# A hybrid decoder layer on one core: the order of the instructions is set by another machine model

## The chip, the core and the metric

The kernel runs on one core of a Trainium2 chip. The metric is the device time of one execution in microseconds (us); the time before is the median of three runs. A core has a matrix engine (TensorE, PE in the profile; its weight loads are shown apart as PEld), VectorE (DVE), ScalarE (ACT), GpSimd (POOL) and SyncE (SP). Each engine takes its instructions strictly in the order in which they stand in its queue and waits at each for the semaphores it needs. Transfers between the chip's memory and the core's on-chip memory are issued from the queues of SP, ACT and POOL.

## The reference

One layer for two groups of tokens at once: a prompt of 512 tokens, and a sample group of 8 sequences with 4 new tokens each, 544 tokens in all, 1024 channels, everything in float32.

```
z = rms_norm(x) @ w_in                                  # 1024 x 3080
za, zb, zc = split(z)
ya = rwkv7(za)            # a recurrence over the tokens, 4 heads of 64
yb = fox(zb)              # attention with forget gates, 8 heads of 64; the prompt over itself,
                          # the sample over 2048 old keys and values in pages of 128 (page_table)
yc = conv_module(zc)      # gated causal convolution of width 31
x += concat(ya, yb, yc) @ w_out
mk, mv = memory(mem_prompt @ w_xk, mem_prompt @ w_xv)   # 256 memory tokens
x += cross_attention(rms_norm(x) @ w_xq, mk, mv) @ w_xo # 4 heads of 256
x += (silu(conv(gate)) * conv(val)) @ w_down            # gate, val = rms_norm(x) @ w_up, 2816 wide
```

The keys, values, gates, states and convolution tails are outputs too.

## The kernel before

The weight products keep the tokens on the free axis: 128 output channels by 272 (or 512) tokens accumulate in one PSUM bank over eight blocks of 128 input channels. Each float32 factor is split into a high and a low part (`split`, L244), and three matmuls make one product of them, high by high, high by low and low by high. `weights` (L267) loads blocks of columns of a weight, ScalarE makes the high part (`w_hi`), VectorE the low (`w_lo`, L247). All matmuls go through `mm` (L185, recorded as L186), transpositions on TensorE through `tr` (L214, L216).

The stages, by the names that the profile and the order show:

- The first product, `bank_g<-act_h` and `act_l` (z = x @ w_in), with three streams beside it: the recurrence's chunks (`rwkv_recurrence`, L896; small matmuls of 64x64 into `bank_r`, on `zbuf`, `RA`, `TR`, `WU`, `G`), the convolution's taps, and the normalisation of keys and queries.
- The prompt's attention, four pairs of heads (`attend`, L1305): scores into `bank_r`, their exponentials in `S0` and `S1`, the transposed weights `PT`, the values.
- The sample's attention over the old keys, one sequence after the other (`sample_past`, L1703). An indirect transfer fetches four pages of keys into `w_raw` (1 MB, two buffers; `four_pages`, L1387, recorded as L1389), VectorE transposes it in blocks of 32 into `KT` (L1404), and 16 matmuls of 128x32 tiles give scores in `bank_s` (`past_scores`, L1394). The values come as `page` (three buffers), and 4 matmuls per page add to `bank_v` (`past_values`, L1448). There are 32 transfers of keys and 32 of values.
- The memory's keys and values, `bank_g<-xT` (`memory`, L1526; the memory's operand lies where the residual `xT` is later), then the output projection of the mixer, `bank_g<-four` with w_out (`out_prompt`, L1629).
- Cross attention: from the first `bank_d` (the query product with w_xq) on. Then the feed-forward, again in `bank_g`.

The program is recorded as several generators side by side. `weave` (L346) takes the next step of the one that is least far along; L1241 weaves the first product, recurrence and convolution, L1726 the sample's attention with everything else up to the output projection (`rest`, L1576). That recording is only a proposal. A scheduler in the library goes through the recorded instructions, and at each step takes, of those that are ready by its own model of the machine, the one of the highest priority, which is the recording position minus what `tc.high_priority(n)` adds. So `urgent` (L350) sets its steps before `n` instructions of the others:

```
def urgent(steps, ahead):
    while True:
        with tc.high_priority(ahead):
            step = next(steps, None)
```

The recurrence is recorded with `ahead` 800 (L1240), the sample's attention with 0 (L1726). `pinned` (L181) can keep instructions in recorded order. Which engine does a copy recorded as `nc.any.tensor_copy` (`anycp`: L1330, L1439, L1524, L1640 and others) is the scheduler's choice as well, and so are the buffer numbers and the semaphore waits that follow from the order.

Of the kernel before, what the change touches and what calls it, by code (L numbers as in the profile page):

```python
# [8 lines left out]
F32 = mybir.dt.float32  # L9
# [34 lines left out]
def _consts():  # L44
    """What depends on shapes alone: identities, masks, selections."""
# [46 lines left out]
    # rows (head, page of four, query) against pages, queries and columns of the like  # L92
# [18 lines left out]
def _past_consts():  # L111
    """of rows (head, page of four, query): causal mask, selections of pages, queries and columns"""
# [14 lines left out]
def _cross_consts():  # L127
    """of rows (head of two, 64 of the keys, token) those of a head and the 64; then selections of 32 rows, four times over"""
    p, m = np.arange(128)[:, None], np.arange(8)[None, :]
    own = [(m // 4 == h) & (m % 4 == p // 32) for h in range(2)]  # L130
    four = [p == 32 * x + np.arange(128)[None, :] % 32 for x in range(4)]
    return np.concatenate(own + four, 1).astype(np.float32)
# [5 lines left out]
def _pack_vectors(x):  # L138
    """Per-channel vectors side by side, a column for each 128 channels."""
# [15 lines left out]
def hybrid_step(tc, A):  # L155
# [62 lines left out]
    def rsqrt_from(out, in_, scale, eps):  # L218
        """out = (in * scale + eps) ** -0.5 by the logarithm and the exponential"""
        act(out=out, in_=in_, func=AF.Ln, scale=scale, bias=eps)  # L220
        act(out=out, in_=out, func=AF.Exp, scale=-0.5)

    def half_xyy(t, y, x, scale, eps):
        """t = (x * scale + eps) / 2 * y ** 2 for y, about the inverse root: (1.5 - t) * y is that root to the last bits"""
# [3 lines left out]
    def rsqrt_rows(out, x, n, scale, eps, eps_ap, work):  # L228
        """out = (x * scale + eps) ** -0.5 for n numbers to a partition"""
# [6 lines left out]
    def neg_sigmoid(t, e):  # L236
        """-1 / (1 + exp(-t)) in place, for t >= -40; by a Newton step"""
# [6 lines left out]
    def split(h, l, src, tt=vtt):  # L244
        """src = h + l exactly, both float32r"""
        acopy(h, src)
        tt(out=l, in0=src, in1=h.bitcast(F32), op=SUB)  # L247

# [18 lines left out]
    def weights(src, kb, cols, width=128, raws=None):  # L267
        """loads blocks of columns, two at most, and returns how to split each"""
# [37 lines left out]
    def gemm_steps(src, cols, xh, xl, evac, bank, spans=EVEN, kb=8, ahead=0, raws=None, first=None):  # L306
        """evac(ps, i, a) for span a of the i-th block of 128 columns; yields what each step costs TensorE"""
# [22 lines left out]
    def woven(*streams, first=False):  # L330
        """several streams side by side, each (its steps, their cost in all, where it sets in), in proportion; to the end of
        all or of the first"""
# [17 lines left out]
    def urgent(steps, ahead):  # L350
        """the steps, each before that many instructions of the others"""
# [27 lines left out]
    # what outlives the phases  # L379
# [16 lines left out]
    def four_blocks(n, dtype=F32R):  # L396
        """the places of four blocks of an operand, high or low"""
        return (yfp, yrp, xkp, xvp)[n].tile([128, 4, NT], dtype, name="four")

    yF = four_blocks(0, F32)  # first holds FoX's queries  # L400
# [5 lines left out]
    cum = cpl.tile([128, SEQ], F32R, name="cum")  # high parts from 0 and 64, low ones from 32 and 96  # L406
# [10 lines left out]
    # ================= inputs, first norm =================  # L417
# [20 lines left out]
    def norm_tok(xt, n, gain, ss, h, l, lo, work, bank, junk):  # L438
        """rows of xt, normed, transposed and split into columns lo.. of h and l"""
# [11 lines left out]
    # the operand is not yet divided by its root mean square: that follows after the products  # L451
# [4 lines left out]
    def roots(lo, n):  # L456
        """1 / root mean square of tokens lo .. lo + n, on all partitions"""
# [43 lines left out]
    # ================= gates of the cached keys =================  # L501
    # one row for each (batch, page), then (batch, head) by key, cumulated from the end
# [28 lines left out]
    # ================= RWKV columns, shifted by a token as they come =================  # L531
# [48 lines left out]
    # ================= RWKV: gates, keys, as their columns come =================  # L580
# [4 lines left out]
    def rmm(lhsT, rhs, evac):  # L585
        """float32 product with all 544 tokens of rhs, by halves"""
# [17 lines left out]
    def gates():  # L604
        """yields how many blocks of columns the next step needs"""
        yield 2
        # tanh(t) = 2 / (1 + exp(-2 t)) - 1
# [6 lines left out]
        # t1: minus the sigmoid of w, t4: that of a  # L614
# [6 lines left out]
        # decays: cumulated in each chunk, centred on half of the chunk's total  # L621
# [7 lines left out]
        # the step to the next chunk's centre, where that chunk's state will lie: [other half, block, head]  # L629
# [11 lines left out]
        # unit keys  # L641
# [40 lines left out]
    # where the cached keys and values lie: of four pages each, partition (page, k) takes rows 4 k .. 4 k + 3  # L682
# [13 lines left out]
    # ================= FoX and conv columns =================  # L696
# [9 lines left out]
    def finish(n=1):  # L706
        """what was put off until n more evacuations"""
# [5 lines left out]
    def evac_fl(ps, i, a):  # L713
        """forget gate: log_sigmoid(y) = -(max(-y, 0) + ln(1 + exp(-|y|)))"""
# [35 lines left out]
    def tok_major(dst, dst_s, src, src_s):  # L750
        """[128 channels, tokens] -> the prompt's token rows and the sample's"""
# [88 lines left out]
    def conv_taps():  # L840
        """the prompt's convolution: some taps on VectorE, the others by ScalarE and GpSimd"""
# [18 lines left out]
    def conv_ahead():  # L860
# [22 lines left out]
        for m in range(2):  # L883
            # the sample's windows, all taps at once: [batch * token, tap], by half the batches
# [11 lines left out]
    def rwkv_recurrence():  # L896
        def group_norm(y, n, heads, ps, work):
            """ps [n, heads, 64] -> y, each row of 64 centred and scaled"""
# [17 lines left out]
        # ================= RWKV: inverses of the blocks of 16 on the diagonals =================  # L916
        # N of (head, block of 128 tokens) as [chunk of two, block of 16, row] by column; with DVE's transposes by blocks
        # of 32 each of the 128 triangles comes to a partition (chunk, half, block of two, head and block of tokens)
# [48 lines left out]
        # ================= RWKV: sample, rows (head, batch, token) =================  # L967
        def sample_steps(rk, rk2):
# [43 lines left out]
            # -alpha S0 and rho S0, each row with its own batch  # L1012
# [37 lines left out]
            # the state after the four tokens  # L1050
# [18 lines left out]
        # ================= RWKV: chunks of 64, two to a block of 128 tokens =================  # L1069
# [4 lines left out]
        def chain(i, j, out):  # L1074
            """what a block and two heads need that no state enters, step by step"""
# [23 lines left out]
            # inverse of I - N by doubling blocks, from those of 16  # L1099
# [43 lines left out]
        def four(t, i):  # L1143
            """a block's columns as [head of two, its block, 64]"""
            return t[:, :, i * 128: (i + 1) * 128].rearrange("p j (r t) -> p j r t", r=2)

        def stateless(i):
            """of a block, in the places of what entered: AT (beta), RP (kap), the outputs (ynT) and the state (values) but for
            what the state before adds"""
# [36 lines left out]
        def stateful(i):  # L1186
            """the state, chunk after chunk: that of chunk ch lies in half ch % 2"""
# [51 lines left out]
    # what of the recurrence is left then runs beside the sample's attention  # L1239
# [38 lines left out]
    def recurrence_end():  # L1278
        """RWKV's group: ((norm * g + b) + bonus) * gate"""
# [9 lines left out]
        # where the residual will lie, the memory's operand  # L1289
# [3 lines left out]
        # causal mask, after nothing for the keys before  # L1293
# [7 lines left out]
    # ================= FoX: the prompt's attention, two heads at a time =================  # L1301
# [895 lines left out]
```

## Time and profile before

| what | value |
|---|---|
| time, median of 3 runs | 1304.64 us (1300.55 to 1308.29) |
| span of the profiled execution, which is its own time from first to last instruction | 1301.6 us |
| TensorE busy; weight loads busy | 1234.1 us; 1011.6 us |
| VectorE, ScalarE, GpSimd busy | 809.1, 501.2, 290.6 us |
| matmul records | 10410 |
| moved by DMA | 173.83 MB, 134 GB/s in the mean |

The span lies 3.0 us under the median. Busy shares are means over stages of different kinds: the first product (to about 320 us), attention of prompt and sample (about 320 to 460), memory and output projection with the rest of the sample's attention (about 460 to 698), cross attention (698 to about 890), feed-forward (to the end). A matmul of float32 data can leave two records in the trace, so the records (10410) are more than the program's matmuls (8376).

### The profile page before, as it was taken

The numbers are of one execution on the slowest core, as the hardware profiler recorded it, in microseconds if no ns is written. First come the engines' busy times: TensorE is split into PE (matmuls) and PEld (weight loads), VectorE is DVE, ScalarE is ACT, GpSimd is POOL, SyncE is SP. The second block draws the span as 40 slices with busy tenths as digits, with TensorE's granted clock in tenths as the row PEclk, the third lists the DMA queues.
The fourth block names the chain that finished last, engine by engine and source line by source line (L and its number), as shares of the span: only waits on it lengthen the run. The fifth ranks groups of instructions, "written<-read, shape, count | busy, mean of one in ns | idle before, by whom it ended". The sixth has DMA issues, their size and how long they took to land.

```text
span 1301.6 us, 24852 instructions
## 1 busy us (share of the span) xinstructions
PE 1234.1 (95%) x10410; PEld 1011.6 (78%) x10410; DVE 809.1 (62%) x1514; ACT 501.2 (39%) x996; POOL 290.6 (22%) x322
## 2 busy tenths in 40 slices
PE   7899899999899999999998988999999999999997
PEld 6788788875555467654447875799999999999996
DVE  4699998765777377453234677557767424777631
ACT  5454543341456435221242422335444323444321
POOL 1262430033342131112223242012111100111120
PEclk9999999997699999999998998999999999999999
DMA  7221220221788497576663465033322323222231
GB/s 227 59 65 51 50 75 19 67 87 44 268 304 304 155 306 244 198 231 226 218 215 118 151 232 174 23 103 98 98 93 60 93 73 127 68 96 88 76 111 48
DMA packets 129649, 173.83 MB, mean 134 GB/s; under 512 B 7029, under 2 KB 110981, under 8 KB 121336
## 3 DMA queue, kind: packets, MB, share of 16 engines
q0 software_dynamic: 15216, 84.80, 18.1%
q1 hardware_dynamic: 88160, 70.76, 17.9%
q10 hardware_dynamic: 26160, 16.66, 4.4%
q8 instruction: 82, 1.34, 0.4%
q14 instruction: 31, 0.25, 0.1%
HBM read 164.54 MB, written 7.88 MB: 132 GB/s over the span
## 4 chain that ended last, share of the span: by engine, by line
PE 77%; DVE 9%; issue 5%; ACT 4%; DMA 3%; POOL 2%; SPq 0%; POOLq 0%; ACTq 0%; DVEq 0%
PE bank_g L186 42%; PE bank_r L186 10%; PE bank_d L186 6%; PE bank_s L186 6%; PE bank_v L186 4%; PE bank_a L186 2%; PE bank_r L216 2%; DVE w_lo L247 1%; PE bank_t L216 1%; PE bank_x L216 1%; DMA w_raw<-in_w_in_dram 1%; DMA w_raw<-in_w_out_dram 1%; DVE four L855 1%; DVE KT L1404 1%; ACT w_hi L177 1%
## 5 line engine op out<-in xcount | busy, mean ns | idle before, releaser
L186 PE MATMUL bank_g<-four,w_hi 128*128 128x272 f32 (+1 forms) x1536 | 284.7, 301 | 2.7 <-ACT w_hi L177 2.0
L177 ACT CAST w_hi<-w_raw 128x1024 fp32r<-128x1024 f32 (+3 forms) x149 | 140.6, 946 | 269.8 <-PE bank_g L186 206.1
L186 PEld LDWEIGHTS bank_g<-four,w_hi 128*128 128x128 f32 x1536 | 222.1, 189 | 26.4 <-issue 19.9
L247 DVE TENSOR_TENSOR w_lo<-w_raw,w_hi 128x1024 fp32r<-128x1024 f32 (+3 forms) x149 | 164.0, 1103 | 87.2 <-ACT w_hi L177 78.2
L186 PE MATMUL bank_g<-four,w_lo 128*128 128x272 f32 (+1 forms) x768 | 173.4, 301 | 0.5 <-DVE w_lo L247 0.5
L186 PEld LDWEIGHTS bank_g<-four,w_lo 128*128 128x128 f32 x768 | 122.1, 189 | 11.3 <-issue 8.6
L186 PE MATMUL bank_g<-act_h,w_hi 128*128 128x272 f32 (+2 forms) x400 | 124.6, 312 | 6.2 <-ACT w_hi L177 2.8
L186 PE MATMUL bank_g<-act_h,w_lo 128*128 128x272 f32 (+2 forms) x400 | 122.9, 308 | 0.0
L186 PE MATMUL bank_g<-act_l,w_hi 128*128 128x272 f32 (+2 forms) x400 | 122.0, 305 | 0.0
L2108 POOL TENSOR_SCALAR ysm<-HS,vec 128x32 f32<-128x32 f32 x44 | 42.0, 954 | 255.1 <-ACT HS L177 255.1
L1404 DVE STREAM_TRANSPOSE KT<-w_raw 128x2048 f32<-128x2048 f32 x32 | 73.5, 2302 | 23.9 <-PE bank_s L186 22.8
L186 PEld LDWEIGHTS bank_g<-act_h,w_hi 128*128 128x128 f32 x400 | 79.5, 199 | 10.5 <-ACT w_hi L177 3.2
L186 PEld LDWEIGHTS bank_g<-act_h,w_lo 128*128 128x128 f32 x400 | 79.1, 198 | 2.8 <-issue 1.2
L186 PEld LDWEIGHTS bank_g<-act_l,w_hi 128*128 128x128 f32 x400 | 79.4, 198 | 2.3 <-issue 1.1
L186 PE MATMUL bank_s<-KT,w_hi 128*32 128x128 f32 x1024 | 76.6, 292 | 3.4 <-DVE rsq L226 1.7
L186 PE MATMUL bank_d<-four,w_hi 128*128 128x272 f32 x384 | 78.1, 299 | 0.0
L186 PE MATMUL bank_g<-in_h,w_hi 128*128 128x272 f32 x352 | 73.6, 290 | 0.0
L186 PE MATMUL bank_g<-in_l,w_hi 128*128 128x272 f32 x352 | 73.5, 290 | 0.0
L186 PE MATMUL bank_g<-in_h,w_lo 128*128 128x272 f32 x352 | 73.2, 289 | 0.0
L186 PE MATMUL bank_v<-page,w_lo 128*32 128x512 f32 x256 | 67.8, 603 | 1.8 <-DMA page<-in_cache_fox_v_dram,kidx 1.8
L186 PEld LDWEIGHTS bank_s<-KT,w_hi 128*32 128x32 f32 x1024 | 39.2, 115 | 32.5 <-issue 19.8
L186 PEld LDWEIGHTS bank_d<-four,w_hi 128*128 128x128 f32 x384 | 61.9, 193 | 1.0
(631 smaller groups left out, 2458.6 us busy)
## 6 DMA issues: line engine op xcount, KB each, us to landing
w_raw<-in_w_up_dram SPq DMA_DIRECT2D x20, 1024.0 KB, 5.1
w_raw<-in_w_down_dram SPq DMA_DIRECT2D x16, 704.0 KB, 4.7
w_raw<-in_w_in_dram SPq DMA_DIRECT2D x17, 512.0 KB, 4.2
w_raw<-in_cache_mem_k_dram SPq DMA_DIRECT2D x16, 512.0 KB, 5.0
sV<-in_cache_mem_v_dram POOLq DMA_DIRECT2D x12, 512.0 KB, 6.4
w_raw<-in_w_in_dram SPq DMA_DIRECT2D x4, 1024.0 KB, 6.6
w_raw<-in_w_xk_dram ACTq DMA_DIRECT2D x8, 512.0 KB, 10.6
w_raw<-in_w_xv_dram ACTq DMA_DIRECT2D x8, 512.0 KB, 10.7
```

Of the source, the lines that this page charges most:

```text
L177: nc.scalar.copy(out, in_)
L186: pinned(nc.tensor.matmul(out, lhsT, rhs, start=start, stop=stop, skip_group_check=True))
L216: pinned(nc.tensor.transpose(out=out, in_=in_, identity=ident[p0:p0 + k, p0:p0 + k]))
L247: tt(out=l, in0=src, in1=h.bitcast(F32), op=SUB)
L855: vstt(out=yp, in0=U[:, m, w: w + SEQ], scalar=w_tap, in1=yp, op0=MUL, op1=ADD)
L1404: nc.vector.transpose(out=KT, in_=K)
L2108: nc.gpsimd.tensor_scalar(out=ysm, in0=H[:, 2:6, 1:], scalar1=w[2], scalar2=b, op0=MUL, op1=ADD)
```

## The change

One argument is added where the kernel's context is made; the scheduler then orders the same recorded instructions against a model that follows the queues and the transfers in time. The diff also takes out the docstrings and comments, with the line numbers kept; two of those places stand for all.

```diff
     def urgent(steps, ahead):
-        """the steps, each before that many instructions of the others"""
+
...
-    with tile.TileContext(nc) as tc:
+    with tile.TileContext(nc, schedule_with_timeline_sim=True) as tc:
         hybrid_step(tc, A)
```

The set of instructions stays: 8376 matmuls, 64 indirect transfers, and so on. 37 of the copies that any engine may do go from VectorE to ScalarE (net; 25 of them at L1439). What changes is the order on each engine and the waits. Counted over the orders: changes of tile shape between neighbouring matmuls fall from 700 to 397, those between 128x32 and 128x128 tiles from 403 to 153; runs of a single key matmul (`bank_s<-KT`) from 98 to 2, of a single value matmul (`bank_v<-page`) from 40 to 4. Of the key matmuls, 224 stood after the memory's first matmul and none do now; of the value matmuls 91, and none now. Of the recurrence's 540 matmuls of 64x64, all stood ahead of the last matmul of the first product and 84 do now.

TensorE's queue in the output projection before; `bank_g` is the projection, `KT` old keys, `page` old values (the last number is a run of equal rows):

```order
L186 MATMUL bank_s_6317<-KT_6324,w_hi_6318 32x128
L186 MATMUL bank_g_6448<-four_5944,w_hi_6449 128x512
L186 MATMUL bank_s_6317<-KT_6324,w_hi_6318 32x128
L186 MATMUL bank_g_6448<-four_5933,w_lo_6450 128x512
L186 MATMUL bank_s_6317<-KT_6324,w_hi_6318 32x128 x3
L186 MATMUL bank_g_6579<-four_5933,w_hi_6580 128x512
L186 MATMUL bank_s_6317<-KT_6324,w_hi_6318 32x128
L186 MATMUL bank_v_6342<-page_6503,w_lo_5995 32x512
```

And where the same keys, `KT_6324`, stand now, between transpositions (`ident`) of the prompt's attention weights `S0` and `S1`:

```order
L216 MATMUL bank_r1_4115<-ident_59,page_4095 128x128 x4
L216 MATMUL bank_r2_4147<-ident_59,S0_4007 128x128 x4
L186 MATMUL bank_s_6317<-KT_6324,w_hi_6318 32x128 x16
L186 MATMUL bank_s_6317<-KT_6390,w_hi_6318 32x128 x14
L216 MATMUL bank_r0_4153<-ident_59,S1_4008 128x128 x4
L186 MATMUL bank_s_6317<-KT_6390,w_hi_6318 32x128 x2
L186 MATMUL bank_v_6055<-page_6056,w_lo_5456 32x512 x4
L216 MATMUL bank_r2_4230<-ident_59,S1_4008 128x128 x3
L186 MATMUL bank_s_6317<-KT_6420,w_hi_6318 32x128 x14
```

The single key matmuls have become runs of 14 and 16, and they no longer stand among the projection's.

TensorE's queue at the first key tiles now, inside the recurrence (`zbuf`, `G`, `TR`, `RA`, `beta`):

```order
L186 MATMUL bank_r1_1816<-beta_389,RA_388 64x64 x2
L186 MATMUL bank_r0_1829<-zbuf0_1305,G0_1751 64x64 x2
L186 MATMUL bank_r0_1829<-zbuf0_1305,G1_1808 64x64 x2
L186 MATMUL bank_r1_1837<-zbuf1_1308,G2_1760 64x64 x2
L186 MATMUL bank_r1_1837<-zbuf1_1308,G3_1817 64x64 x2
L186 MATMUL bank_s_3676<-KT_3727,w_hi_3677 32x128 x15
L186 MATMUL bank_r0_1829<-zbuf0_1305 64x64 x8
L186 MATMUL bank_r1_1837<-zbuf1_1308 64x64 x8
L186 MATMUL bank_s_3676<-KT_3727,w_hi_3677 32x128
```

Before, no key matmul stood ahead of the recurrence's last one; now 384 of 512 do, in runs between the recurrence's steps.

VectorE's queue at the first key transposition (L1404) before, where the prompt's scores (`S0`, `S1`) of the first heads are already being taken:

```order
L755 COPY four_113<-bank_x_3591 128x4x128
L1299 ISA S0_4007,st_4006<-bank_r2_4051,tri_3995 128x384
L1299 ISA st_4006 128x1
L1299 ISA S1_4008,st_4006<-bank_r0_4052,tri_3995 128x384
L1299 ISA st_4006 128x1
L1404 STREAM_TRANSPOSE KT_3683<-w_raw_3679 128x2048
L1404 STREAM_TRANSPOSE KT_3705<-w_raw_3701 128x2048
L1299 ISA S0_4007,st_4006<-bank_r1_4061,tri_3995 128x512
L1299 ISA st_4006 128x1
```

and now, where recurrence rows (`beta`, `kap`, `XS`, `zb`, `G0`) stand on both sides:

```order
L1164 TENSOR_TENSOR beta_389<-cf_60,bank_r2_1573 128x2x128
L1167 TENSOR_TENSOR kap_390<-RA_388,bank_r2_1573 64x2x64 x4
L1197 TENSOR_TENSOR XS_1120<-zb_357,ev_392 64x256
L1404 STREAM_TRANSPOSE KT_3683<-w_raw_3679 128x2048
L1404 STREAM_TRANSPOSE KT_3705<-w_raw_3701 128x2048
L1196 TENSOR_TENSOR zb_357<-bank_r2_1894,zb_357 64x2x128
L1382 TENSOR_TENSOR Sn_3623<-bank_k_3640,cpf_3621 128x32
L226 SCALAR_TENSOR_TENSOR rsq1_4100<-mss_4093,rsq1_4100 128x1
L1096 TENSOR_TENSOR G0_1751<-bank_r0_1750,cf_60 128x320
L1197 TENSOR_TENSOR XS_1120<-zb_357,ev_392 64x256
```

The first transposition stood after 513 rows of VectorE's order and stands after 364 now.

GpSimd's queue, which issues the indirect transfers of keys (`w_raw`) and values (`page`), from the third key transfer on, before:

```order
L1389 DMA w_raw_3723<-in_cache_fox_k_dram,kidx_95 128x2048
L1389 DMA w_raw_3779<-in_cache_fox_k_dram,kidx_95 128x2048
L1389 DMA page_4265<-in_cache_fox_v_dram,kidx_95 128x2048
L1389 DMA w_raw_3890<-in_cache_fox_k_dram,kidx_95 128x2048
L1389 DMA w_raw_4029<-in_cache_fox_k_dram,kidx_95 128x2048
L1389 DMA page_4340<-in_cache_fox_v_dram,kidx_95 128x2048
L1389 DMA w_raw_4071<-in_cache_fox_k_dram,kidx_95 128x2048
```

and now:

```order
L1389 DMA w_raw_3723<-in_cache_fox_k_dram,kidx_95 128x2048
L1389 DMA page_4265<-in_cache_fox_v_dram,kidx_95 128x2048
L1389 DMA w_raw_3779<-in_cache_fox_k_dram,kidx_95 128x2048
L1389 DMA w_raw_3890<-in_cache_fox_k_dram,kidx_95 128x2048
L1389 DMA w_raw_4029<-in_cache_fox_k_dram,kidx_95 128x2048
L1389 DMA w_raw_4071<-in_cache_fox_k_dram,kidx_95 128x2048
L1389 DMA w_raw_4122<-in_cache_fox_k_dram,kidx_95 128x2048
```

Keys now run ahead of the values: 17 value transfers stand before the last key transfer, where 24 stood before.

The queue of SP keeps its order but for the places of a few loads, and the feed-forward's order is the same on all engines.

## Rows read from the trace of the kernel before

**Rows 1.** The page's part 1: busy us, share of the span, instructions

```profile
PE 1234.1 (95%) x10410; PEld 1011.6 (78%) x10410; DVE 809.1 (62%) x1514; ACT 501.2 (39%) x996; POOL 290.6 (22%) x322
```

**Rows 2.** Table by stretch: length, PE, PEld, DVE, ACT, POOL, PEclk, DMA, GB/s

```profile
100.00:125.00 25.00, 23.41 (x225) 21.85 (x224) 23.63 (x41) 10.51 (x15) 3.65 (x7) 1.00 0.26 66
175.00:330.00 155.00, 151.52 (x1790) 119.27 (x1789) 112.10 (x271) 51.73 (x131) 34.69 (x39) 0.93 0.21 61
330.00:469.00 139.00, 131.12 (x1184) 74.44 (x1183) 93.45 (x186) 72.56 (x199) 43.02 (x41) 0.93 0.72 259
469.00:698.00 229.00, 218.75 (x1439) 126.26 (x1438) 108.33 (x197) 71.26 (x149) 46.59 (x42) 0.99 0.64 220
698.00:893.00 195.00, 182.43 (x1707) 155.32 (x1707) 117.87 (x225) 68.07 (x147) 47.05 (x56) 0.96 0.42 139
893.00:1260.00 367.00, 367.00 (x2946) 366.04 (x2945) 225.82 (x356) 141.96 (x219) 53.49 (x64) 1.00 0.29 88
325.00:350.00 25.00, 21.70 (x214) 14.36 (x215) 17.17 (x33) 8.65 (x25) 9.34 (x13) 0.57 0.80 276
375.00:400.00 25.00, 22.50 (x218) 11.78 (x216) 22.39 (x45) 18.16 (x48) 9.16 (x8) 1.00 0.86 329
```

**Rows 3.** Timeline of weight loads, two places; start us, us, [idle before]

```profile
590.79 0.14 PEld L186 LDWEIGHTS bank_s<-KT,w_hi 128*32 128x32 f32 x2 [0.24 <-issue]
...
591.55 0.14 PEld L186 LDWEIGHTS bank_s<-KT,w_hi 128*32 128x32 f32 x2 [0.24 <-issue]
...
604.61 0.14 PEld L186 LDWEIGHTS bank_v<-page,w_lo 128*32 128x32 f32 x2 [0.24 <-issue]
...
606.01 0.14 PEld L186 LDWEIGHTS bank_v<-page,w_lo 128*32 128x32 f32 x2 [0.24 <-issue]
```

**Rows 4.** The chain of waits, 640 to 690 us; start us, us, what

```profile
642.54 0.33 PE bank_v L186 x2
...
645.59 1.01 PE bank_s L186 x32
...
653.73 6.84 issue
...
660.80 6.92 DMA page<-in_cache_fox_v_dram,kidx
...
672.22 3.00 PE bank_g L186 x12
675.21 0.99 PE bank_v L186 x8
```

**Rows 5.** Waits of the weight loads, 450 to 698; total us, times, longest

```profile
PEld bank_g L186 <- issue: 42.2, 122, 0.8
PEld bank_s L186 <- issue: 16.4, 56, 2.2
PEld bank_v L186 <- issue: 13.2, 39, 0.8
```

**Rows 6.** Waits of POOL, 330 to 470 us, the longest

```profile
POOL w_raw L1389 <- DVE KT L1404: 29.7, 7, 9.8
```

**Rows 7.** Lines L1389 and L1404, 280 to 440 us; ns min/median/max, starts

```profile
L1389 POOL DMA_INDIRECT w_raw<-in_cache_fox_k_dram,kidx x14: 997/1004/1273, 346.0 to 420.0; - x14
L1389 POOL DMA_INDIRECT page<-in_cache_fox_v_dram,kidx x10: 1002/1004/1221, 340.2 to 424.4; - x10
...
DMA to landing us min/median/max: 5.6/7.9/9.6
...
L1404 DVE STREAM_TRANSPOSE KT<-w_raw x18: 2267/2306/2311, 330.3 to 439.6; 128x2048 f32<-128x2048 f32 x18
```

**Rows 8.** Instructions on act_h, xT and bank_d on PE, first and last start

```profile
L186 PE MATMUL bank_g<-act_h,w_hi x400: 276/289/609, 12.7 to 319.3; 128*128 128x272 f32 x91, 128*128 128x256 f32 x22, 128*128 128x288 f32 x21
...
L186 PE MATMUL bank_g<-xT,w_hi x256: 275/282/469, 458.5 to 554.0; 128*128 128x256 f32 x128
...
L186 PE MATMUL bank_d<-four,w_hi x384: 283/288/492, 697.9 to 884.0; 128*128 128x272 f32 x192
```

## The prediction

> **What bounds the kernel now.** I read the page's busy row first, then a table by stretch, then the stretches that looked strange, instruction by instruction. TensorE is busy for 1234.1 of 1301.6 us [rows 1]; taken at its word only 67.5 us could be gained. The table by stretch shows what hides in that [rows 2]. From 893 to 1260 us TensorE takes 2946 matmuls in 367 us (0.125 us each) and its weight loads are busy for 366. From 469 to 698 it is as "busy" (219 of 229), yet passes 1439 matmuls (0.159 us each) and loads weights for 126 us only. The Trainium skill's page "Trainium Kernel Development and Optimization" (Performance Expectations) says that matmul busy time is a bad measure, since matmuls are pipelined, and that the busy share of the weight loads is a good one. By the busy row the stretch 469 to 698 has 10 us to give, by the weight loads up to 229 - 126 = 103; the rows that follow side with the page.
>
> Those rows are single weight loads in that stretch [rows 3]: a matmul on a 128x32 tile (bank_s from KT, the old keys) stands between two on a 128x128 tile (bank_g, the weight products), and each change of shape leaves 0.24 us in which the load waits for nothing that the profile shows. One key and one weight product together take 591.55 - 590.79 = 0.76 us; with a value matmul (bank_v from page) in the key's place 606.01 - 604.61 = 1.40. Kept apart they are cheap [rows 4]: 16 key matmuls (32 loads) 1.01 us, so 0.063 each; 12 weight products 3.00, 0.25 each; 4 value matmuls (8 loads) 0.99, 0.25 each. All such waits of the stretch 450 to 698 come to 42.2 + 16.4 + 13.2 = 71.8 us [rows 5].
>
> Elsewhere another engine leads. At 100 to 125 us VectorE is busy 23.6 of 25 us [rows 2]: it paces the first product. The 64 transfers of old keys and values start in earnest at 340 us; 14 of keys and 10 of values go out from 340.2 to 424.4 [rows 7], so one every 84.2 / 23 = 3.66 us, while the table has 259 to 329 GB/s. The key transfers wait for their buffer: POOL stands 29.7 us for VectorE's transposition KT [rows 6].
>
> **The change part by part.** No instruction is new. 37 small copies go from VectorE to ScalarE; at VectorE's mean of 112.10 / 271 = 0.41 us [rows 2] that is 15 us at most on engines that have gaps, and I count it as nothing. The cross attention, feed-forward and end keep their order nearly or wholly: nothing, within the 12.6 us that TensorE idles from 698 to 893 [rows 2], of either sign. What moves lies ahead of 698 us.
>
> First, the recurrence moves behind the first product. Of its 64x64 matmuls, all 540 that the order shows ahead of the last matmul of that product stood there before; 84 do now. In loads, 1245 fewer stand ahead of it; at 155 / 1790 = 0.087 us [rows 2] that is 108 us of TensorE. VectorE binds here, however: ahead of the first key transposition there were 513 rows of its order and now there are 364, and 149 x 0.41 = 61 us. I take the smaller, 60, because VectorE's row is the fuller one. The third key transfer then goes out at 346 - 60 = 286 us.
>
> Second, keys and values come during the recurrence. From there 30 key and 32 value transfers are left; 17 values stand ahead of the last key. At the measured 3.66 us the last key goes out at 286 + 47 x 3.66 = 458, is there and transposed (7.9 to land, 2.3 [rows 7]) at 468, and the last value arrives at 286 + 62 x 3.66 + 7.9 = 521. After the last key 444 loads are left before the memory's product; at 139 / 1184 = 0.117 us [rows 2] that is 52: 520. TensorE's own count is later: the product ends at 319 - 108 = 211 [rows 8], and 1245 loads at 0.087 and 1853 at 0.117 follow: 536. I take 525, between the two, for the memory's first product, which was at 458.5 [rows 8].
>
> Third, what is left of the stage from there to the first cross-attention matmul (697.9 - 458.5 = 239.4 us [rows 8]). 224 key and 91 value matmuls are gone from it: 224 x 0.063 = 14 and 91 x 0.25 = 23. The alternation goes with them: of 98 key matmuls that stand alone between other shapes 85 lie after 450 us, of 40 value matmuls 30. A key saves 0.76 - 0.25 - 0.063 = 0.45, together 38. A value saves between 0.33 - 0.25 = 0.08 (one in the chain, [rows 4]) and 1.40 - 0.50 = 0.90, together 2 to 27; I take 18, nearer to the upper end, for 56 in all, under the 71.8 of the waits. The wait for the last pages of values, 6.84 + 6.92 = 13.8 us [rows 4], goes, since all values are now ahead of that point. 239.4 - 14 - 23 - 56 - 13.8 = 132.6.
>
> The sum: cross attention starts at 525 + 132.6 = 657.6 instead of 697.9, 40.3 us earlier. The profiled execution's 1301.6 becomes 1261.3; the runs' median lies 3.0 above it, so 1264. With 520 and the full 65 of the alternation it is 1250, with 536 and only 40 it is 1291.
>
> A stall goes only if its cover holds. TensorE's queue is in order, so in the new stretch a key matmul that waits for its transfer holds back the recurrence matmul behind it, and the recurrence's rows on VectorE hold back the transposition that frees the next transfer's buffer. Late next is the transfer rate itself.
>
> **Rivals.**
> 1. *Keys come one at a time; slower.* Two buffers take the old keys, and VectorE's order now puts recurrence rows between transpositions, each of which waits for TensorE. If that undoes the double buffer, a key costs issue, landing and transposition in turn, 1.0 + 7.9 + 2.3 = 11.2 us [rows 7]: 286 + 30 x 11.2 + 52 + 132.6 = 807, 109 us late, 1413. It decides from (697.9 - 132.6 - 52 - 286) / 30 = 7.6 us a key; halfway, at 9.4, it gives 1359. For it speaks that POOL waited for KT 7 times already; against it, that with VectorE at 22.4 of 25 us the transfers still moved 329 GB/s [rows 2]. The Trainium skill's page "SBUF — State Buffer" (the "DVE blocks DMA" trap) says that transfers issued by GpSimd starve while VectorE runs a two-port operation. These transfers are GpSimd's, and the change puts them beside more VectorE work, so that rule would lead here too; at 375 to 400 us no run of this kernel shows it.
> 2. *TensorE at half clock.* From 325 to 350 us, where recurrence ended and the heads began, with waits between small matmuls, the granted clock was 0.57 [rows 2]: of 25 us, 10.8 were lost. Were the first 75 us after the product like that, 32 of the 40 us would go: 1296.
> 3. *No change.* The alternation's gaps covered waits for transfers, and these come back as plain waits: of the 40 us all but a few are eaten at a key cadence of about 7.5 us. 1298 to 1311.
> 4. *More.* VectorE does not bind the first product and all 108 us come through: the third key at 238, the memory's product at 472, and with the full 65 the cross attention at 596: 1203.
> That the change does nothing is excluded by the orders.
>
> **Chances.** My forecast (1238 to 1288) 0.48; more than that (below) 0.15; the clock or part of the waits (1288 to 1298) 0.07; no change 0.1; slower 0.2. A measurement of this kernel tells about 0.5% (6.5 us) from no change. So faster 0.7, same 0.1, slower 0.2. The range that leaves 2 in 10 outside: 1212 to 1335, which takes in the bounds of the sum, most of rival 4 and the lower part of rival 1; the forecast's own is 1238 to 1288.
>
> **What would show it.** Right: the first memory product near 525 us and the first cross-attention matmul near 658; the loads' waits for nothing shown falling from 71.8 us to under 20 in the stage before it; key transfers going out from about 286 us at 6 us apart or less in the mean while recurrence matmuls still run; the wait for pages gone; the feed-forward's length unchanged. Wrong: key transfers more than 7.6 us apart, VectorE standing for TensorE between transpositions, a granted clock under 0.7 after the first product, or a first product that still ends near 319.

## The result, and the profile after

The changed kernel takes 1282.48 us (median of four, 1279.53 to 1285.69) against 1303.14 of the kernel before on the same chip: a ratio of 0.984, 95% interval 0.981 to 0.987. The profiled execution's span is 1278.6 us, 23.0 under before's 1301.6. The forecast was 1264, a gain of 40; the direction and the range came out, and of the size about half.

TensorE's busy row, the one that the argument set aside, fell by 78 us while the time fell by 23 [rows 1]:

```profile
PE 1155.8 (90%) x10410; PEld 996.8 (78%) x10410; DVE 792.2 (62%) x1477; ACT 512.5 (40%) x1033; POOL 283.0 (22%) x322
```

First and last starts on the landmarks of [rows 8], and the recurrence's last product beside them, from the same view of the kernel after:

```profile
L186 PE MATMUL bank_g<-act_h,w_lo x400: 274/288/498, 15.6 to 232.2; 128*128 128x272 f32 x91, 128*128 128x256 f32 x22, 128*128 128x288 f32 x21
...
L186 PE MATMUL bank_r<-S0T,TKs x8: 587/822/1110, 421.9 to 434.9; 32*64 32x512 f32 x8
...
L186 PE MATMUL bank_g<-xT,w_hi x256: 274/282/580, 547.3 to 602.4; 128*128 128x256 f32 x128
...
L186 PE MATMUL bank_d<-four,w_hi x384: 283/288/574, 673.2 to 861.5; 128*128 128x272 f32 x192
```

The first product ends at 232 instead of 319 us, the memory's product starts at 547 instead of 458.5, cross attention at 673.2 instead of 697.9. What was won in the first stage (87 us) was lost in the second, which takes 315 us instead of 139, and the third made the gain: 125.9 us instead of 239.4. The table by stretch, with the columns of [rows 2], cut at the new landmarks:

```profile
250.00:345.00 95.00, 73.88 (x1333) 52.43 (x1329) 73.86 (x146) 31.15 (x102) 27.86 (x27) 0.91 0.77 277
345.00:450.00 105.00, 74.48 (x801) 36.93 (x802) 47.34 (x106) 23.32 (x74) 33.01 (x31) 0.70 0.59 202
547.00:673.00 126.00, 118.48 (x796) 101.58 (x796) 66.48 (x101) 49.30 (x82) 13.38 (x11) 0.93 0.41 115
868.00:1235.00 367.00, 366.78 (x2943) 365.52 (x2942) 224.64 (x354) 143.95 (x222) 51.16 (x61) 1.00 0.28 87
```

From 547 to 673 the weight loads are busy for 102 of 126 us, where they were for 126 of 229; the feed-forward is as it was. From 345 to 450 no engine is near full: TensorE is busy 71% of the time, VectorE 45%, and the granted clock is 0.70 in the mean. The waits there, of POOL and of the weight loads (us in total, times, longest; the first two from 232 to 547 us, the third from 232 to 673):

```profile
POOL page L1389 <- PE bank_v L186: 70.9, 25, 7.2
POOL w_raw L1389 <- DVE KT L1404: 40.1, 11, 7.5
...
PEld bank_v L186 <- DMA page<-in_cache_fox_v_dram,kidx: 26.9, 10, 9.8
```

Transfers wait for buffers, and buffers for TensorE, which waits for transfers. The alternation's own waits are gone: where the loads of bank_g, bank_s and bank_v waited 71.8 us for nothing shown [rows 5], 1.7 us of it are left between 547 and 673, and the longest wait there is for the high parts of weights:

```profile
PEld bank_g L186 <- ACT w_hi L177: 8.8, 3, 4.9
...
PEld bank_s L186 <- issue: 1.7, 2, 1.4
```

The key transfers (the view of [rows 7]), from 248 to 346 and from 346 to 457 us:

```profile
L1389 POOL DMA_INDIRECT w_raw<-in_cache_fox_k_dram,kidx x20: 1002/1005/1173, 247.4 to 345.5; - x20
L1389 POOL DMA_INDIRECT page<-in_cache_fox_v_dram,kidx x7: 1002/1002/1067, 248.9 to 342.6; - x7
DMA to landing us min/median/max: 6.1/7.0/8.2
...
L1389 POOL DMA_INDIRECT w_raw<-in_cache_fox_k_dram,kidx x11: 1002/1008/1112, 345.5 to 456.4; - x11
L1389 POOL DMA_INDIRECT page<-in_cache_fox_v_dram,kidx x10: 997/1003/1078, 359.9 to 448.0; - x10
```

The key at 345.5 stands in both views. 20 keys go out in 98 us, 5.2 apart, then 10 more in 111, 11.1 apart. In the first part a key's round trip is the chain itself (the chain of waits, start, us, what):

```profile
295.50 8.03 DMA w_raw<-in_cache_fox_k_dram,kidx
303.62 2.31 DVE KT L1404
...
306.20 7.31 DMA w_raw<-in_cache_fox_k_dram,kidx
```

### The profile page after: what moved, and what is told of

Same layout as the page of the kernel before. It is cut to its first block, busy times and chain, and to the rows that moved or that the text cites. A ratio compares the mean times of both kernels' runs of the same rounds, so it can differ in the third digit from the quotient of the medians.

```text
span 1278.6 us, 24839 instructions
## 1 busy us (share of the span) xinstructions
PE 1155.8 (90%) x10410; PEld 996.8 (78%) x10410; DVE 792.2 (62%) x1477; ACT 512.5 (40%) x1033; POOL 283.0 (22%) x322
## 4 chain that ended last, share of the span: by engine, by line
PE 61%; DMA 12%; DVE 11%; issue 9%; ACT 4%; POOL 2%; SPq 0%; ACTq 0%; POOLq 0%; DVEq 0%
PE bank_g L186 41%; PE bank_d L186 6%; PE bank_r L186 6%; DMA w_raw<-in_cache_fox_k_dram,kidx 6%; DMA page<-in_cache_fox_v_dram,kidx 3%; DVE four L855 2%; PE bank_v L186 2%; DMA w_raw<-in_cache_mem_k_dram 2%; PE bank_s L186 2%; PE bank_a L186 1%; DVE w_lo L247 1%; DVE KT L1404 1%; DVE sKT L1884 1%; PE bank_t L216 1%; DMA x_tok<-in_x_prompt_dram 1%
## 5 line engine op out<-in xcount | busy, mean ns | idle before, releaser
L186 PE MATMUL bank_g<-four,w_hi 128*128 128x272 f32 (+1 forms) x1536 | 275.2, 298 | 5.6 <-ACT w_hi L177 4.7
L186 PE MATMUL bank_g<-act_h,w_hi 128*128 128x272 f32 (+2 forms) x400 | 121.9, 305 | 8.4 <-DVE fraw L768 4.7
L186 PE MATMUL bank_g<-act_h,w_lo 128*128 128x272 f32 (+2 forms) x400 | 119.3, 298 | 0.0
L186 PE MATMUL bank_g<-act_l,w_hi 128*128 128x272 f32 (+2 forms) x400 | 119.3, 298 | 0.0
L2108 POOL TENSOR_SCALAR ysm<-HS,vec 128x32 f32<-128x32 f32 x44 | 41.6, 946 | 253.4 <-ACT HS L177 253.4
L1404 DVE STREAM_TRANSPOSE KT<-w_raw 128x2048 f32<-128x2048 f32 x32 | 73.6, 2305 | 21.2 <-DMA w_raw<-in_cache_fox_k_dram,kidx 17.4
L186 PE MATMUL bank_v<-page,w_lo 128*32 128x512 f32 x256 | 46.2, 698 | 23.5 <-DMA page<-in_cache_fox_v_dram,kidx 23.3
L186 PE MATMUL bank_s<-KT,w_hi 128*32 128x128 f32 x1024 | 50.5, 313 | 15.4 <-DVE KT L1404 9.3
L2100 DVE TENSOR_TENSOR up<-bank_g,tot 128x544 f32<-128x544 f32 x44 | 31.7, 722 | 44.7 <-PE bank_g L186 44.6
```

The lines of the kernel that those rows point to most:

```text
L186: pinned(nc.tensor.matmul(out, lhsT, rhs, start=start, stop=stop, skip_group_check=True))
L1404: nc.vector.transpose(out=KT, in_=K)
L2100: vtt(out=two(x[:, 2:]), in0=ev2(ps), in1=two(rstd), op=MUL)
L2108: nc.gpsimd.tensor_scalar(out=ysm, in0=H[:, 2:6, 1:], scalar1=w[2], scalar2=b, op0=MUL, op1=ADD)
```

## The experiments

Times are medians; "E1" and so on are the experiments in their order. The kernel before, run beside each, had medians of 1303 to 1306 us. One table has the landmarks of every profiled execution, in us: the end of the first product (last start on act_h with w_lo), the recurrence (first start of zbuf with G to last of S0T with TKs), the start of the memory's product and of cross attention, and the span.

| kernel | time | product ends | recurrence | memory | cross att. | span |
|---|---|---|---|---|---|---|
| before | 1303 | 319.5 | 176.8 to 309.9 | 458.5 | 697.9 | 1301.6 |
| after | 1282 | 232.2 | 216.5 to 434.9 | 547.3 | 673.2 | 1278.6 |
| E1 keys and values in runs | 1259 | 318.8 | 174.5 to 308.4 | 459.8 | 653.4 | 1258.1 |
| E2 after, first stage as recorded | 1327 | 355.8 | 139.0 to 405.7 | 555.9 | 717.2 | 1324.8 |
| E3 after, few values | 1276 | 232.3 | 216.5 to 446.7 | 538.1 | 663.5 | 1273.4 |
| E4 before, few values | 1310 | 313.5 | 173.6 to 305.1 | 453.9 | 701.5 | 1300.4 |
| E5 E1, recurrence late | 1337 | 227.8 | 240.9 to 505.5 | 601.6 | 732.1 | 1336.4 |
| E6 after, few keys and values | 1233 | 230.8 | 215.0 to 404.4 | 497.3 | 623.9 | 1230.6 |
| E7 E1, few keys and values | 1218 | 319.8 | 175.1 to 309.3 | 454.8 | 615.3 | 1215.3 |
| E8 E1, recurrence even | 1312 | 341.2 | 175.0 to 414.3 | 527.2 | 699.4 | 1303.0 |
| E9 after, keys behind recurrence | 1289 | 233.1 | 217.4 to 337.1 | 485.9 | 683.3 | 1291.9 |
| E10 E1, attention ahead | 1254 | 321.4 | 174.3 to 308.1 | 435.8 | 649.3 | 1251.2 |
| E11 before, keys alone in runs | 1267 | 316.4 | 176.7 to 308.1 | 449.7 | 660.3 | 1261.6 |
| E12 after, product held back | 1284 | 310.7 | 159.1 to 382.0 | 522.3 | 675.9 | 1282.5 |

**E1, the alternation alone.** In the kernel before, the matmuls of keys and values get precedence as they are recorded (scheduled by the old model, the rest of the order hardly moves):

```diff
-    mm(acc[po, pg * 128: (pg + 1) * 128], Qx[:, 4 * hp + x].rearrange("p m q -> p (m q)"), KT[:, :, 4 * hp + x], pg == 0 and x == 0, False)
+    with tc.high_priority(400):
+        mm(acc[po, pg * 128: (pg + 1) * 128], Qx[:, 4 * hp + x].rearrange("p m q -> p (m q)"), KT[:, :, 4 * hp + x], pg == 0 and x == 0, False)
...
-    mm(acc[po], PT[:, j, pg * 32: pg * 32 + 32], t[:, j * 512: j * 512 + 512], pg == 0, False)
+    with tc.high_priority(400):
+        mm(acc[po], PT[:, j, pg * 32: pg * 32 + 32], t[:, j * 512: j * 512 + 512], pg == 0, False)
```

Expected: 

> The kernel before, with the 16 key matmuls of a tile and the 4 value matmuls of a page put 400 instructions ahead, so that they stand in runs; single key matmuls fall from 98 to 0, single value matmuls from 40 to 6, the recurrence and the first product keep their places. Theory A (the gain is the alternation of tile shapes; moving the recurrence behind the first product gives most of it back in the stretch of keys and values): 1240 to 1265 us, the first cross-attention matmul 40 to 60 us before 698. Rival B (the alternation's gaps only covered waits for transfers; the gain comes from the earlier transfers): 1290 to 1305 us.

Measured: 1259.46 us, ratio 0.9665 (0.960 to 0.973), better than the change. Cross attention starts 44.5 us earlier, all of it after 459.8, where the alternation stood. In E1's timeline of weight loads a tile's keys are one piece with one gap on each side, where 0.24 us stood beside each pair [rows 3]:

```profile
563.27 0.19 PEld L186 LDWEIGHTS bank_g<-four,w_hi 128*128 128x128 f32 x1
563.83 0.81 PEld L186 LDWEIGHTS bank_s<-KT,w_hi 128*32 128x32 f32 x32 [0.36 <-issue]
564.84 0.19 PEld L186 LDWEIGHTS bank_g<-four,w_hi 128*128 128x128 f32 x1 [0.20 <-issue]
```

Theory A's first half stands: in the old order the alternation costs 44 us. The change removes it too and gains 21, so, if it is worth as much in the new order (no run puts it back there), the new order loses some 20 elsewhere.

**E2, the kernel after with the first stage in recorded order.** `pin[0] = True` stands before the weave of L1241 and `False` behind it.

Expected: 

> The kernel after, but TensorE's instructions of the first product, recurrence and convolution stay in recorded order: 504 of the 540 recurrence matmuls again stand ahead of the first product's last matmul, while keys and values stay in runs (8 and 14 single ones). Theory A: the first product ends near 310 to 320 us again, the stretch of keys and values is no longer thin, and the whole takes 1245 to 1270 us, under the 1282 of the kernel after. Rival B (early transfers are the gain): 1295 to 1310 us. Rival C (the half clock in the thin stretch is all that was lost): the granted clock is above 0.9 from the first product's end to the memory's product, and the time 1250 to 1265 us.

Measured: 1326.83, ratio 1.018 (1.012 to 1.025). No theory had that. The granted clock from the product's end to the memory's product was 0.85, so rival C's condition was not met. The rigid order made the first stage itself slow (its product ends at 356, and TensorE is busy 10.5 to 15.5 us in four of its stretches of 25), and the recurrence takes 267 us, with its last part among the keys again, so the total does not part the theories. From the product's end to cross attention it takes 361 us, against 441 in the kernel after and 378 before.

**E3 and E4, few values.** 24 of 32 value transfers are left out of the kernel after (E3) and before (E4):

```diff
-    t = four_pages(page(), "cache_fox_v", b, pg)
+    t = four_pages(page(), "cache_fox_v", b, pg) if pg == 0 else t
```

Expected of E3: 

> The kernel after with 24 of the 32 value transfers left out (each sequence's first page is used four times). Theory A (the stretch from 231 to 547 us waits for the round trips of transfers): 30 to 60 us under the kernel after, 1222 to 1252 us, since weight loads and matmuls of values waited 26.9 and 23.3 us for pages there. Rival D (VectorE or TensorE's work binds that stretch): within 12 us of the kernel after, 1270 to 1283 us.

Expected of E4: 

> The kernel before with the same 24 value transfers left out. Theory A (before, transfers lie beside TensorE's alternation): the 13.8 us wait for the last pages goes and little more, 1285 to 1302 us. Rival B (transfers bind there too): 1240 to 1275 us.

Measured: E3 1275.77 (ratio 0.977, 0.971 to 0.984), 7 under the kernel after, in D's range; E4 1310.00 (1.005, 1.002 to 1.008), slightly over before and in neither range. So the waits for pages that fill the profile after (26.9 us on the loads) are not what its stretch costs; theory A is wrong there. In E4 the loads of bank_g, bank_s and bank_v still wait 73.7 us for nothing shown between 450 and 702 us: the alternation stayed, and leaving out the last pages won nothing. The recurrence in E3 took 230 us, no less than the 218 of the kernel after, although the last key went out at 403.8 instead of 456.4. That led to theory F: the recurrence crawls, because key tiles stand between its steps, and attention and the memory's product follow its end.

**E5 and E8, the recurrence moved in E1.** `urgent(rwkv_recurrence(), 800)` becomes -1500 (E5, nearly the place it has in the kernel after) and 0 (E8).

Expected of E5: 

> The kernel of the grouping experiment (1259 us), with the recurrence set 1500 instructions behind instead of 800 ahead: 33 of its 540 matmuls stand ahead of the first product's last matmul, as 84 do in the kernel after, and all keys and values stand ahead of the memory's product, as there. Theory F (the kernel after is grouping minus the price of a recurrence moved out of the first product): 1272 to 1300 us, first product's end near 235, recurrence from about 215 to 400 us or later. Rival G (the place of the recurrence is neutral, and the kernel after loses by other moves): 1250 to 1265 us.

Expected of E8: 

> The kernel of the grouping experiment with the recurrence 0 instead of 800 instructions ahead: 492 of its 540 matmuls stay ahead of the first product's last matmul, and keys begin a little earlier in TensorE's order. Theory F: the first product ends 5 to 15 us earlier and the recurrence as much later, 1252 to 1272 us. Rival G (its place is neutral): the same 1259 us within 5.

Measured: E5 1337.19 (1.025, 1.020 to 1.029), 78 over E1, and E8 1311.88 (1.008, 1.004 to 1.012), 52 over. The sign is F's, the size far above what it was given. In E5 the product ends 91 us earlier and the recurrence 197 later. But E5, with the alternation gone and the recurrence nearly where the kernel after has it, takes 55 us more than the kernel after; F's sum, grouping minus the price of the moved recurrence, does not give that kernel its time. In E8, whose ten runs lie between 1304 and 1323, the product ends 22 us later and not 5 to 15 earlier; the recurrence starts at the same 175 us and ends at 414 instead of 308, with its last part among the keys.

**E6 and E7, few keys and values.** In the kernel after (E6) and E1 (E7), 24 of 32 key transfers with their transpositions are left out (`if pg == 0:` before the load and the transposition), and the 24 value transfers as in E3; the matmuls stay.

Expected of E6: 

> The kernel after with 24 of the 32 key transfers and their transpositions and 24 of the 32 value transfers left out (each sequence's first tile is used four times; the matmuls stay). Theory F (the recurrence crawls there because each of its steps queues behind key tiles that wait for transfers and transpositions): the recurrence, 216 to 435 us in the kernel after, takes 130 to 170 us, and the whole 1195 to 1240 us. Rival H (the recurrence alone, without the first product beside it, is that slow by its own chain and the low clock): it still takes over 190 us, and the whole 1250 to 1276 us.

Expected of E7: 

> The kernel of the grouping experiment with the same key and value transfers left out. Theory F: there the recurrence is done before the keys come, so only transfers at the end of the stage can bind: 1235 to 1257 us. Rival (transfers bind there as much as in the kernel after): a fall as large as that of the kernel after, 1195 to 1225 us.

Measured: E6 1233.45 (0.944, 0.938 to 0.950), E7 1218.00 (0.934, 0.930 to 0.937): 49 and 41 us less. E6's total is F's, but its recurrence still takes 189 us, between the two theories, and TensorE is busy for 180.7 of them with 2886 records (168.0 of 218 with 2481 in the kernel after): with less to wait for, more of the other work comes between its steps. E7 is against F: where the recurrence is long done, transfers and transpositions together bind as much. E6 has its gain ahead of the memory's product (50 us); E7 has 5 there and 33 behind it. So the transfers cost both kernels 40 to 50 us, in different stages.

**E9, keys behind the recurrence, in the kernel after.** The rest of the recurrence is recorded before the sample's attention; `behind` sets the TensorE and VectorE instructions of that attention (by `tc.issue_after`) behind the last ones recorded until then:

```diff
+    weave((recurrence, 48.0), (conv_work, 48.0))
...
-    weave((urgent(sample_past(), 0), 135.0), (rest(), 148.0, 0.06))
+    weave((behind(sample_past()), 135.0), (rest(), 148.0, 0.06))
```

Expected: 

> The kernel after, with the sample's attention (TensorE's and VectorE's part) set behind the last instruction of the recurrence, so that the recurrence, which still stands behind the first product (84 of 540 matmuls ahead of its end), has no key tiles between its steps. Theory F (key tiles between its steps slow the recurrence, 218 us in the kernel after): it takes 135 to 160 us there, the first product still ends near 232, the memory's product starts at 470 to 510 instead of 547, and with keys and values left over for later the whole takes 1255 to 1290 us. Rival H (without the first product beside it the recurrence is slow by its own chain and the low clock): it still takes 180 us or more, and the whole 1290 to 1330 us.

Measured: 1289.41 (0.987, 0.983 to 0.991), in F's range but no gain over the kernel after. The recurrence itself answers clearly: 120 us instead of 218. The stretches of the recurrence in E9 and in the kernel after, in this order (columns of [rows 2]):

```profile
217.00:337.00 120.00, 95.53 (x1428) 73.16 (x1428) 60.05 (x171) 29.42 (x81) 16.77 (x22) 0.79 0.13 38
```

```profile
217.00:435.00 218.00, 167.99 (x2481) 111.23 (x2479) 137.49 (x291) 63.99 (x199) 66.28 (x69) 0.82 0.63 221
```

The granted clock is nearly the same, 0.79 and 0.82, so a low clock does not make it crawl: the keys and values that come between its steps do (1053 more matmul records in the stretch), with their transfers and transpositions. E9 takes all of these out together and does not part them. But the memory's product comes only 61 us earlier (486 for 547), and the keys and values left over lengthen the stage behind it to 197 us, from 126. What is pushed out of one stage is paid in the next.

**E10, E1 with the prompt's attention 800 ahead.** `urgent(prompt_attention(), 800)` in `rest`.

Expected: 

> The kernel of the grouping experiment with the prompt's attention 800 instructions ahead, so that the chain from the recurrence to the memory's product has precedence over keys and values (272 key and 96 value matmuls then stand behind the memory's first matmul, 192 and 80 in the grouping experiment). If that chain sets the time: the memory's product 20 to 40 us before 460, and 1235 to 1255 us. If TensorE's and the transfers' work sets it there: what is gained is lost behind it, 1255 to 1268 us.

Measured: 1254.43 (0.962, 0.956 to 0.968). The memory's product starts 24 us earlier and cross attention 4; the chain to the memory is not what sets E1's time. The time itself lies where the two expected ranges meet, and its interval overlaps E1's. Both beat the change.

**E11, keys alone in runs.** Only the first half of E1's edit.

Expected: 

> The kernel before with only the key matmuls put in runs; single value matmuls stay. By the prediction's terms keys are worth 38 of 56 us: 1262 to 1280 us, between the kernel before and the grouping experiment (1259). If values carry most of it: 1280 to 1295 us.

Measured: 1266.78 (0.971, 0.967 to 0.976): 37 to 39 us for the keys, and by the difference to E1 5 to 7 for the values; there the intervals of E1 and E11 overlap, so the values' share is not clear of noise.

**E12, the kernel after with the product held back loosely.** Each step of the first product is set (`tc.issue_after`) behind TensorE's recurrence instructions recorded eight of the recurrence's steps earlier.

Expected: 

> The kernel after, with each step of the first product set behind the recurrence's TensorE instructions that were recorded eight of its steps earlier, and nothing else held (a looser hold than keeping the recorded order): 488 of the 540 recurrence matmuls stand ahead of the first product's last matmul, keys and values stay in runs (8 and 3 single ones). If the recurrence's place is what the kernel after lost against the grouping experiment (1282 against 1259): the first product ends at 305 to 330 us, the stretch from there to the first cross-attention matmul takes 335 to 365 us instead of 441, and the whole 1250 to 1275 us. If the other moves of the new order lose it: 1282 us or more.

Measured: 1284.03 (0.987, 0.981 to 0.993), the time of the kernel after. The product ends at 311, as asked, and the stretch behind it falls to 365 us, just outside what was expected; 79 lost, 76 won. The recurrence still ends at 382, with its last part among the keys. So having most of the recurrence inside the product is no gain under the new model; in every kernel that reached 1267 or less with all its transfers it was over by 310 us, before the first key.

## Why the prediction was right and where it failed

*The alternation, term 56, under the waits' 71.8.* Right in kind, and by E1 large enough for the whole gain: 44 us when it alone goes. Keys were given 38 and measured 37 to 39; values were given 18 and measured 5 to 7, within noise. The lower price of a value, 0.33 us, was misread: the timeline shows that those rows of [rows 4] are products with new values (`vs`) on a 32x32 tile, and not with `page`:

```profile
642.47 0.40 PE L186 MATMUL bank_v<-vs,PnT 32*32 32x128 f32 x2
```

The upper price, 1.40 us a pair, was read rightly but is not won in full. With the values in runs too, the loads wait longer for pages: between 450 and 702 us 10.7 us in E1, 4.2 in E11 and 2.2 before.

*The wait for the last pages, term 13.8.* This term failed. The chain followed a transfer, but TensorE worked on the projection meanwhile: it was busy for 12.3 of those 14.0 us, and its loads waited 2.19 us for the page (columns of [rows 2], then the timeline of the loads):

```profile
653.70:667.70 14.00, 12.32 (x58) 6.21 (x56) 4.44 (x11) 6.53 (x16) 6.11 (x5) 1.00 0.51 171
...
667.77 0.16 PEld L186 LDWEIGHTS bank_v<-page,w_lo 128*32 128x32 f32 x8 [2.19 <-DMA page<-in_cache_fox_v_dram,kidx]
```

E4, without most of these transfers, was no faster than before.

*The third stage, 132.6.* Measured 125.9, but by luck. E1's third stage still takes 193.6 us; without the 14 and 23 us of the keys and values that moved it would be 157, and 31 us more went that the sum did not name. E1's loads of bank_g, bank_s and bank_v still wait 24.6 us there for nothing shown and 10.7 for pages, and the kernel after has next to none of either; no run shows that these are the 31.

*The first product, 60 us earlier.* Measured 87. VectorE did not bind as supposed: up to the product's end (0 to 320 us before, 0 to 232 now) TensorE's busy time fell from 295.5 to 205.0 us and VectorE's from 246.2 to 192.7, so the end moved with TensorE's work. The key at 346 us was the fifth; the third went out at 336.1 before and at 247.4 now, 89 us earlier and in step with the product. The forecast had 286.

*The last key at 458, transposed by 468.* Measured 456.4 and 468.3, but by two errors that cancel: the transfers started 39 us sooner than forecast and came 7.2 us apart in the mean (209 us for 29) instead of 5.7. For the first 98 us the forecast rate held, 3.8 us a transfer; from 345 on it did not.

*The memory's product at 525.* This step failed: 547. The sum asked what the transfers need and what TensorE needs, and took a place between the two (520, 536). It left out the serial chain. The attention's buffers are opened when the recurrence's are closed (`recurrence_end`, L1278), and its first scores on VectorE (L1299) come 15 us after the recurrence's last product before, 10 now, and 5 to 16 in E1, E5, E6 and E9. The recurrence, 133 us beside the first product, takes 218 among the keys, and 112 us lie between its end and the memory's product. Behind the last transposed key 52 us had been counted, and 79 passed. E9 shows the crawl's cause by taking keys and values away (120 us). The prediction has the chain in its paragraph "A stall goes only if its cover holds", with no price. So cross attention came at 673.2 and not at 657.6: 22 us late by the memory's product, 7 early by the third stage.

*Rival 1, keys one at a time, deciding at 7.6 us a key.* It came half true: 7.2 us a key. The Trainium skill's page "SBUF — State Buffer" (the "DVE blocks DMA" trap) says that GpSimd's transfers starve while VectorE runs a two-port operation. No run here tests it: no row shows whether VectorE's work beside these transfers, mostly stream transpositions (41.6 of 73.9 us from 250 to 345), is of that kind. A transfer landed in 7.0 us in the median there, against 7.9 in [rows 7], whose transfers are those from 340 to 432 us.

*Rival 2, the clock.* It is there: 0.70 in the mean from 345 to 450, between the two levels of 1.2 and 2.4 GHz, with TensorE busy 71% and waiting. E9 had the fast recurrence at 0.79. What the clock costs that stretch was not tried.

*Rival 4* had most of its first half (87 of 108 us at the product) and not its second.

Of the signs, the loads' waits fell, the feed-forward kept its length and the first product no longer ends near 319; the keys' pace, 7.2 us, missed the 6 and stayed under the 7.6.

Open: why the new order, with the alternation gone as in E1, needs 23 us more. Shown is that a recurrence that ends among the keys goes with a longer time (E5 and E8, against E1, E10 and E11), and that taking the keys out of it (E9) or putting most of it back (E2, E12) moves the loss to the neighbouring stage. That it is the cause of these 23 us is not shown. A version of the new order with the whole recurrence over before the first key, as E1 has it, was not among the runs.

## What to carry to other kernels

Count changes of tile shape in TensorE's order before looking at busy shares: a stretch where single 128x32 and 128x128 matmuls alternate reads as 95% busy, and putting them in runs is two lines of priority. When a scheduler moves a serial chain from beside dense work to beside work that itself waits, give the chain its own term in the sum, with every foreign instruction between its steps. A scheduler's better model of the machine is one change of many orders at once: try alone the one thing that it improves, which here was worth 44 us against 21. Before counting a wait of the chain as time to be won, look whether the engine that sets the time worked meanwhile.

## What the runs showed of the hardware

A single 128x32 matmul between 128x128 ones cost about 0.45 us over its place in a run (an estimate: 37 to 39 us in E11 over the 85 keys that stood alone after 450 us), and TensorE's busy row counts that time as work: from 575 to 600 us before, where they alternate, it is busy for 25.0 of 25 us, the weight loads for 10.7. The granted clock was 0.70 in the mean over 105 us in which TensorE was busy 71% of the time; a stretch of small recurrence matmuls ran in 120 us at 0.79.
